# First loads in the order of use, two more banks for the third tile, the norm's steps at set places, and tables moved later, in a decoder trunk on one core

## The chip, the cores and the metric

The kernel runs on one core of one Trainium2 chip. The core has five engines with a queue each: TensorE (PE, with its weight loads PEld), VectorE (DVE), ScalarE (ACT), GpSimd (POOL) and SyncE (SP), which here only issues DMAs. Operands lie in SBUF, matmuls write to PSUM, which has eight banks of 512 float32 columns. The metric is the device time of one launch in microseconds (us); lower is better.

## The reference, cut to what matters

A trunk of two layers over 256 tokens of width 1024, in float32. Each layer has a SwiGLU feed-forward block, a mixer, and a second such block; the change touches what stands around the first block.

```python
def rms_norm(x, g):
    y = xf * lax.rsqrt(jnp.mean(xf * xf, axis=-1, keepdims=True) + EPS)
    return y * g

def swiglu(x, w_gate, w_up, w_down):
    return (jax.nn.silu(x @ w_gate) * (x @ w_up)) @ w_down      # 1024 -> 2816 -> 1024

for layer in range(2):
    if layer == 1:
        shared_kv = shared_moba_kv(h, positions, kv_norm_g, w_kv, k_norm_g)
    h = h + 0.5 * swiglu(rms_norm(h, ffn1_norm_g[layer]), ...)
    hn = rms_norm(h, mix_norm_g[layer])
    # layer 0: convolution module and attention to a memory of 256 rows
    # layer 1: attention over shared_kv (rotary, causal) and attention to the memory
    h = h + concatenate([primary, mem_out]) @ w_o[layer]
    h = h + 0.5 * swiglu(rms_norm(h, ffn2_norm_g[layer]), ...)
```

## The kernel before, in words

Everything is held transposed: channels on the partitions, the 256 tokens on the free axis. All weights come in one stream of chunks of 128 x 2048 float32 (1 MB) that SP loads in the order of use into three buffers (`raw`). Each chunk has two halves of 1024 columns, and each half is split in two: ACT rounds it (`wh`, L186), DVE takes the rest (`wl`, L190). A product with a tile of 128 x 128 weights is then three products in two matmuls (`mm2`, the "triple" of the title): `wh` on both parts of y side by side (512 columns), and `wl` on y's high part (256 columns). Four buffers hold `wh` halves and four `wl` halves.

The four feed-forward blocks are called a, b, c, d (`ffn`). Such a block has 22 tiles j of 128 hidden channels; a tile is a gate pass and an up pass of eight triples each (one for each k, the tile of input channels), into one PSUM bank each (`ag`, `au`, or `bg`, `bu` and so on). Four banks of the tag "mm" turn in rotation; two more have the tag "sc" and two the tag "aux". A bank comes free when ACT has copied its one half (`ags0c`, L237) and DVE has added the halves (`ags`, `ah`, L239). Then DVE scales the gate with the norm (L331), ACT applies Silu (L333), and the product with the up half is split again into `hs` (L336 to L338), the input of the down pass (`ao`).

The RMS norm of a block is applied after its gate product. The squares are summed over the channels (`aacc`), two small matmuls give means as columns (`mean_cols`, `anrp`), DVE and GpSimd make the reciprocal roots (`anr`), and `bcast_rows` spreads them over the partitions with two transposes (`anbp`) and a copy (`anb`). Before, the mean is taken after tile 0 of the block and the rows are made inside tile 2 (`TURN_J`), after the first matmul of triple 4 (`TURN_K`); where a turn is put inside a triple, its transposes stand between the triple's two matmuls.

The beginning is special. Warm-up matmuls (`WARM`) run on constants. x and the first chunk are loaded in pieces, two of x's from ACT's queue, and y is x times the gain, made tile by tile by ACT and DVE by turns (`scaled_split`). Tiles 0 and 1 of block a run together: the first two chunks hold, for each k, the four weight tiles of `ag0, au0, ag1, au1`. The squares of x stand on ACT beside it.

`prepare` is called before each tile of block a from tile 2 on. At tile 5 it loads the vectors, the positions, the gains and the memory, makes tables (masks in bf16, cosine and sine), squares the memory and sums it on GpSimd (`macc`); at tile 9 it makes the memory's keys and values (`mkv`). In the down passes of a, b and c a few transposes are placed that nobody reads (`unread`, at `pauses`).

A tile scheduler sets the order of the instructions of each engine from the program's order and its own costs; DMAs of SP run in the order of its queue. Everything after tile 15 of block a keeps its order on all engines apart from the places that the diff names.

Of the kernel before, what the change touches and what calls it, by code (L numbers as in the profile page):

```python
# [40 lines left out]
WARM = 12  # L41
# [12 lines left out]
TURN_J = 2  # L54
TURN_K = 4
# [30 lines left out]
def tile_kernel(ctx: ExitStack, tc: tile.TileContext, w, xT, memT, pos, vec, hg, const, out):  # L86
# [27 lines left out]
    nc.sync.dma_start(x[:, :2], xT[:, :2])  # L114
    nc.sync.dma_start(raw0[:, :HC // 2], w[0][:, :HC // 2])
    nc.scalar.dma_start(x[:, 4:6], xT[:, 4:6])
    nc.sync.dma_start(x[:, 2:4], xT[:, 2:4])
    nc.sync.dma_start(raw0[:, HC // 2:HC], w[0][:, HC // 2:HC])
    nc.scalar.dma_start(x[:, 6:], xT[:, 6:])
    nc.sync.dma_start(raw0[:, HC:], w[0][:, HC:])  # L120
# [109 lines left out]
    def mm_group2(o, y, turn=None):  # L230
        for k, wt in enumerate(tiles_of(1)):
            mm2(o, wt, y, k, k == 0, k == KD - 1, turn if k == TURN_K else None)

# [87 lines left out]
    def ffn(name, y, acc, nexts, store=False, both=False, hook=None, after=None, hook_down=None, r=None, turns=(),  # L321
            pauses=(), n_pause=2):
# [4 lines left out]
        turns = list(turns)  # L327
        halves = {}

# [10 lines left out]
        for j in range(KF):  # L340
# [4 lines left out]
            if first and j == 0:  # L345
# [7 lines left out]
                nc.scalar.dma_start(cst, const)  # L353
# [14 lines left out]
            else:  # L368
                pg, pu = psum(f"{name}g{j}"), psum(f"{name}u{j}")
                if j == 0:  # L370

                    wts = [list(tiles_of(1)) for _ in range(2)]
                    for ks in (range(KD - 1), (KD - 1,)):
                        for o, wt in zip((pg, pu), wts):
                            for k in ks:
                                mm2(o, wt[k], y, k, k == 0, k == KD - 1)
                else:
                    turn = None
                    if j == TURN_J and rb is None:
                        def turn():  # L380
                            state["rb"] = bcast_rows(name + "nb", r)
                    elif j >= TURN_J and turns:
                        turn = turns.pop(0)
                    mm_group2(pg, y, turn)
                    mm_group2(pu, y)
            if j == 0 and r is None:
                r = rstd_cols(name + "nr", acc)
            if rb is None and j < TURN_J:
                halves[j] = both_halves(f"{name}gs{j}", pg, "g"), both_halves(f"{name}h{j}", pu, "h")
                continue  # L390
            if rb is None:
                rb = state["rb"]
            for i in sorted(halves):
                gated(i, *halves.pop(i), rb)
            gated(j, both_halves(f"{name}gs{j}", pg, "g"), lambda: both_halves(f"{name}h{j}", pu, "h"), rb)
        if after:
            tables(after)
        def unread():

            pk = psum(f"{name}pk", "aux", 2)  # L400
            for i in range(n_pause):
                transp(pk[:, i * P:(i + 1) * P], ident, ident)

# [3 lines left out]
        for m in range(KD):  # L407
# [294 lines left out]
    for k in range(KD):  # L702
        scaled_split(y, x[:, k], k, V_FFN1, k % 2 == 1)
    kv0 = []

    def prepare(j):
# [3 lines left out]
        if j != 5:  # L710
            return
        nc.sync.dma_start(vt[:, V_TAP:], vec[:, V_TAP:])
        nc.sync.dma_start(pt, pos)
        nc.sync.dma_start(gt, hg)
        nc.sync.dma_start(mT, memT)
        nc.vector.tensor_copy(identb, ident)
        nc.vector.tensor_tensor(ident2, ident[:, :HALF_CH], ident[:, HALF_CH:], op=ALU.add)
        nc.vector.tensor_copy(maskb, cst[:, C_MASK:C_MASK + P])

        for g, n in ((G_MQ, 2), (G_Q, 1)):  # L720
            gn = gt[:, g * HD:(g + n) * HD]
            nc.vector.tensor_scalar(gn, gn, -1.0, None, op0=ALU.mult)

        posf = cp.tile([P, NT], F32, name="posf")
        nc.vector.tensor_copy(posf, pt)
        ang = cp.tile([P, NT, HALF], F32, name="ang")
        for i in range(NT):
            nc.vector.tensor_scalar(ang[:, i], cst[:, C_FREQ:C_FREQ + HALF], posf[:, i:i + 1], None, op0=ALU.mult)
        for shift, dst in ((0.25, cosT), (0.0, sinT)):
            kk = tp.tile([P, NT, HALF], F32, name="kk", tag="kk")  # L730
            nc.vector.tensor_scalar(kk, ang, 1.0 / TWO_PI, shift, op0=ALU.mult, op1=ALU.add)
            nc.vector.tensor_scalar(kk, kk, ROUND, ROUND, op0=ALU.add, op1=ALU.subtract)
            rr = tp.tile([P, NT, HALF], F32, name="rr", tag="rr")
            nc.vector.scalar_tensor_tensor(rr, kk, -PI_1, ang, op0=ALU.mult, op1=ALU.add)
            nc.vector.scalar_tensor_tensor(rr, kk, -PI_2, rr, op0=ALU.mult, op1=ALU.add)
            nc.vector.scalar_tensor_tensor(rr, kk, -PI_3, rr, op0=ALU.mult, op1=ALU.add)
            if shift:
                nc.vector.tensor_scalar(rr, rr, TWO_PI / 4, None, op0=ALU.add)
            nc.vector.tensor_scalar(rr, rr, 3.1415925, -3.1415925, op0=ALU.min, op1=ALU.max)
            nc.scalar.activation(dst[:, :, HALF:], rr, AF.Sin)  # L740
            if shift:
                nc.vector.tensor_copy(dst[:, :, :HALF], dst[:, :, HALF:])
            else:
                nc.vector.tensor_scalar(dst[:, :, :HALF], dst[:, :, HALF:], -1.0, None, op0=ALU.mult)

# [14 lines left out]
    def diagonals(m):  # L760
        for i in range(m * 4 * SHIFTS // KD, (m + 1) * 4 * SHIFTS // KD):
# [5 lines left out]
                    pauses=((1, 12),))  # L767
# [243 lines left out]
    (ykv, y), acc = ffn("b", y, acc, (V_KV, V_FFN1 + KD), pauses=((1, 12),), n_pause=1)  # L1011
# [9 lines left out]
    (y,), acc = ffn("c", y, acc, (V_MIX + KD,), after=AF.Exp, r=rkv, turns=turns, pauses=((1, 12), (4, 4)))  # L1021
# [40 lines left out]
    ffn("d", y, acc, (), store=True)  # L1062
# [126 lines left out]
```

## Time and profile before

| what | value |
|---|---|
| runs | 993.52, 994.16, 994.66 us (median 994.16) |
| profiled execution | 996.29 us, of which the span 994.2 |
| PE busy | 979.8 us (99%) |
| DVE, ACT, POOL busy | 734.3, 593.1, 128.4 us |
| HBM read, written | 171.43 MB, 1.05 MB |
| mean granted clock of TensorE | 0.993 |

Times in the trace are counted from the start of the span. The granted clock is 1 at 2.4 GHz and 0.5 at 1.2 GHz. A timeline row gives start, length, engine, line, operation, what it writes and reads, how many were merged, and in brackets the idle time of its engine before it with what ended it; matmuls are pipelined, so that starts and not lengths give their pace.

### The profile page before, as it was taken

How to read it: one execution, taken by the hardware profiler on the slowest of the kernel's cores; microseconds unless marked ns; L12 is line 12 of the kernel's file. 1: busy time of each engine (PE TensorE's matmuls, PEld its weight loads, DVE VectorE, ACT ScalarE, POOL GpSimd, SP SyncE). 2: the span in 40 equal slices, each digit the busy share in tenths (PEclk: the TensorE clock that was granted, in tenths of full speed). 3: DMA queues.
4: the chain of work that ended last, by engine and by line, in shares of the span. 5: the costliest groups of instructions: out<-in, count | busy, mean ns of one | idle time of the engine just before them, and what ended most of it. 6: DMA issues, size and time to landing. Idle time of an engine off the chain costs nothing.

```text
span 994.2 us, 15549 instructions
## 1 busy us (share of the span) xinstructions
PE 979.8 (99%) x5791; PEld 851.8 (86%) x5791; DVE 734.3 (74%) x1322; ACT 593.1 (60%) x1151; POOL 128.4 (13%) x150
## 2 busy tenths in 40 slices
PE   8999999999999999999999999999998999999998
PEld 6888888898779888888888888888995798888887
DVE  7887776679967877777776877767787588777663
ACT  6676578757666655555556655555555656555542
POOL 0202000128813000000122000000152030000000
PEclk9999999999999999999999999999997999999999
DMA  9555554533324555554554555555541055555560
GB/s 328 196 189 197 176 205 170 206 134 128 104 108 175 206 192 190 175 205 171 194 188 173 199 179 199 183 194 187 174 174 78 3 189 212 191 186 196 177 225 22
DMA packets 26427, 173.47 MB, mean 174 GB/s; under 512 B 3184, under 2 KB 4592, under 8 KB 6000
## 3 DMA queue, kind: packets, MB, share of 16 engines
q1 hardware_dynamic: 25776, 171.79, 49.1%
q8 instruction: 45, 0.74, 0.3%
q10 hardware_dynamic: 576, 0.70, 0.2%
q14 instruction: 30, 0.25, 0.1%
HBM read 171.43 MB, written 1.05 MB: 173 GB/s over the span
## 4 chain that ended last, share of the span: by engine, by line
PE 90%; ACT 3%; DVE 3%; POOL 2%; DMA 1%; issue 1%; SPq 0%; ACTq 0%; POOLq 0%; DVEq 0%
PE cg L150 7%; PE bg L150 6%; PE bu L150 6%; PE do L150 6%; PE ao L150 6%; PE bo L150 6%; PE co L150 6%; PE dg L150 6%; PE cu L150 6%; PE du L150 6%; PE au L150 5%; PE ag L150 5%; PE kv L150 3%; PE oao L150 2%; PE obo L150 2%; PE mkv L150 2%
## 5 line engine op out<-in xcount | busy, mean ns | idle before, releaser
L186 ACT ACTIVATE wh<-raw 128x1024 fp32r<-128x1024 f32 (+1 forms) x307 | 324.1, 1057 | 309.2 <-PE dg L150 27.7
L190 DVE TENSOR_TENSOR wl<-raw,wh 128x1024 fp32r<-128x1024 f32 (+1 forms) x307 | 377.5, 1231 | 174.9 <-ACT wh L186 173.7
L150 PE MATMUL ag<-y,wh 128*128 128x512 f32 x176 | 64.0, 399 | 3.1 <-ACT wh L186 2.9
L150 PE MATMUL au<-y,wh 128*128 128x512 f32 x176 | 63.6, 397 | 1.3 <-DVE ags L239 1.3
L150 PE MATMUL bg<-oay,wh 128*128 128x512 f32 x176 | 63.5, 399 | 0.0
L150 PE MATMUL bu<-oay,wh 128*128 128x512 f32 x176 | 63.4, 398 | 0.0
L150 PE MATMUL dg<-oby,wh 128*128 128x512 f32 x176 | 62.5, 393 | 0.0
L150 PE MATMUL cg<-by,wh 128*128 128x512 f32 x176 | 62.3, 393 | 0.0
L150 PE MATMUL du<-oby,wh 128*128 128x512 f32 x176 | 62.3, 392 | 0.0
L150 PE MATMUL cu<-by,wh 128*128 128x512 f32 x176 | 62.2, 392 | 0.0
L150 PE MATMUL ao<-ahs,wh 128*128 128x512 f32 (+1 forms) x198 | 62.0, 369 | 0.0
L150 PE MATMUL do<-dhs,wh 128*128 128x512 f32 (+1 forms) x198 | 61.9, 369 | 0.0
L150 PE MATMUL co<-chs,wh 128*128 128x512 f32 (+1 forms) x198 | 61.9, 369 | 0.0
L150 PE MATMUL bo<-bhs,wh 128*128 128x512 f32 (+1 forms) x198 | 61.9, 369 | 0.0
L150 PE MATMUL ao<-ahs,wl 128*128 128x256 f32 x176 | 49.7, 283 | 0.0
L150 PE MATMUL co<-chs,wl 128*128 128x256 f32 x176 | 49.7, 283 | 0.0
L150 PE MATMUL do<-dhs,wl 128*128 128x256 f32 x176 | 49.7, 283 | 0.0
L150 PE MATMUL bo<-bhs,wl 128*128 128x256 f32 x176 | 49.6, 283 | 0.0
L150 PE MATMUL ag<-y,wl 128*128 128x256 f32 x176 | 49.6, 283 | 0.0
L150 PE MATMUL au<-y,wl 128*128 128x256 f32 x176 | 49.5, 282 | 0.0
L150 PE MATMUL bg<-oay,wl 128*128 128x256 f32 x176 | 49.5, 281 | 0.0
L150 PE MATMUL cg<-by,wl 128*128 128x256 f32 x176 | 49.5, 281 | 0.0
(1001 smaller groups left out, 2441.2 us busy)
## 6 DMA issues: line engine op xcount, KB each, us to landing
raw<-in_w SPq DMA_DIRECT2D x158, 1024.0 KB, 4.8
raw<-in_w SPq DMA_DIRECT2D x5, 512.0 KB, 7.4
mT<-in_memT SPq DMA_DIRECT2D x1, 1024.0 KB, 8.3
out<-x SPq DMA_DIRECT2D x8, 128.0 KB, 1.7
x<-in_xT SPq DMA_DIRECT2D x2, 256.0 KB, 4.5
x<-in_xT ACTq DMA_DIRECT2D x2, 256.0 KB, 5.3
raw<-in_w SPq DMA_DIRECT2D x2, 256.0 KB, 5.1
gt<-in_hg SPq DMA_DIRECT2D x1, 192.0 KB, 6.3
```

Source lines behind the costliest of these rows:

```text
L150: return in_order("P", nc.tensor.matmul(*a, **k))
L186: state["act"] = nc.scalar.activation(wh[:, s], raw[:, s], AF.Copy)
L190: state["dve"] = nc.vector.tensor_tensor(wl[:, s], raw[:, s], wh[:, s].bitcast(F32), op=ALU.subtract)
```

## The change

The loads of x and of the first chunk are issued by SP alone, in the order in which they are used: one tile of x, the 512 columns for it, the next of both, then larger pieces. The first two chunks are split in halves of 512 columns throughout. DVE instead of ACT makes y for even tiles. The sums of tile 2 of block a go to the two "sc" banks, and their halves are added after the norm's rows are there. A plan says for each block in which tile, pass and triple the mean, the rows and other turns stand: block a has the mean in tile 2 and the rows in tile 3, block b's rows come one triple later. The memory's squares move from tile 5 to tile 8, the masks to tile 12, the cosine and sine tables to tile 14; their loads stay at tile 5. The unread transposes go, and two of the twelve warm-up matmuls. The load of the constants is put behind the last split of the first two chunks.

```diff
-WARM = 12
+WARM = 10
...
-    nc.sync.dma_start(x[:, :2], xT[:, :2])
-    nc.sync.dma_start(raw0[:, :HC // 2], w[0][:, :HC // 2])
-    nc.scalar.dma_start(x[:, 4:6], xT[:, 4:6])
-    nc.sync.dma_start(x[:, 2:4], xT[:, 2:4])
-    nc.sync.dma_start(raw0[:, HC // 2:HC], w[0][:, HC // 2:HC])
-    nc.scalar.dma_start(x[:, 6:], xT[:, 6:])
-    nc.sync.dma_start(raw0[:, HC:], w[0][:, HC:])
+    q = HC // 2
+    for tiles, cols in ((slice(0, 1), slice(0, q)), (slice(1, 2), slice(q, HC)), (slice(2, 4), slice(HC, CH)),
+                        (slice(4, KD), None)):
+        nc.sync.dma_start(x[:, tiles], xT[:, tiles])
+        if cols is not None:
+            nc.sync.dma_start(raw0[:, cols], w[0][:, cols])
...
-        q = HC // 2 if n == 0 and h == 0 else HC
+        q = HC // 2 if n < 2 else HC
...
-                nc.scalar.dma_start(cst, const)
+                behind(nc.scalar.dma_start(cst, const), state["act"])
...
-                pg, pu = psum(f"{name}g{j}"), psum(f"{name}u{j}")
+                at = ("sc", 2) if first and j == 2 else ()
+                pg, pu = psum(f"{name}g{j}", *at), psum(f"{name}u{j}", *at)
...
-                    mm_group2(pg, y, turn)
-                    mm_group2(pu, y)
+                    mm_group2(pg, y, planned(j, "g"))
+                    mm_group2(pu, y, planned(j, "u"))
...
-                    mm2(po, next(it), hs, k, k == 0, k == KF - 1, unread if (m, k) in pauses else None)
+                    mm2(po, next(it), hs, k, k == 0, k == KF - 1)
...
-        scaled_split(y, x[:, k], k, V_FFN1, k % 2 == 1)
+        scaled_split(y, x[:, k], k, V_FFN1, k % 2 == 0)
...
-        if j != 5:
-            return
+        if j == 12:
+            nc.vector.tensor_copy(identb, ident)
...
+        if j == 14:
+            posf = cp.tile([P, NT], F32, name="posf")
...
+        if j == 5:
+            nc.sync.dma_start(vt[:, V_TAP:], vec[:, V_TAP:])
+            nc.sync.dma_start(pt, pos)
+            nc.sync.dma_start(gt, hg)
+            nc.sync.dma_start(mT, memT)
+        if j != 8:
+            return
         macc = tp.tile([P, SEQ], F32, name="macc", tag="macc", bufs=1)
...
-                    pauses=((1, 12),))
+                    plan={(2, "u", 1): "mean", (3, "g", 3): "rows"})
...
-    (ykv, y), acc = ffn("b", y, acc, (V_KV, V_FFN1 + KD), pauses=((1, 12),), n_pause=1)
+    (ykv, y), acc = ffn("b", y, acc, (V_KV, V_FFN1 + KD), plan={(2, "g", 5): "rows"})
...
-    (y,), acc = ffn("c", y, acc, (V_MIX + KD,), after=AF.Exp, r=rkv, turns=turns, pauses=((1, 12), (4, 4)))
+    (y,), acc = ffn("c", y, acc, (V_MIX + KD,), after=AF.Exp, r=rkv,
+                    plan={(2 + i, "g", 4): turn for i, turn in enumerate(turns)})
...
-    ffn("d", y, acc, (), store=True)
+    ffn("d", y, acc, (), store=True, plan={(2, "g", 4): "rows"})
```

The first place is ACT's queue at the beginning, from the first y on. `wh0_0` is the first half of the first chunk, `sq0` the squares of x. Before:

```order
L275 ACTIVATE y0_110<-x_74,vt_71 128x256
L186 ACTIVATE wh0_0_139<-raw0_95 128x512
L353 DMA cst_70<-in_const 128x264
L275 ACTIVATE y0_110<-x_74,vt_71 128x256
L357 ACTIVATE sq0_226<-x_74 128x256 x4
L275 ACTIVATE y0_110<-x_74,vt_71 128x256
L357 ACTIVATE sq0_226<-x_74 128x256 x2
L275 ACTIVATE y0_110<-x_74,vt_71 128x256
L357 ACTIVATE sq0_226<-x_74 128x256 x2
L186 ACTIVATE wh0_0_139<-raw0_95 128x512
L186 ACTIVATE wh0_1_161<-raw0_95 128x1024
```

And now:

```order
L366 ACTIVATE sq0_230<-x_74 128x256
L183 ACTIVATE wh0_0_137<-raw0_93 128x512
L272 ACTIVATE y0_108<-x_74,vt_71 128x256
L366 ACTIVATE sq0_230<-x_74 128x256
L183 ACTIVATE wh0_0_137<-raw0_93 128x512
L272 ACTIVATE y0_108<-x_74,vt_71 128x256
L366 ACTIVATE sq0_230<-x_74 128x256 x2
L183 ACTIVATE wh0_1_159<-raw0_93 128x512 x2
L272 ACTIVATE y0_108<-x_74,vt_71 128x256 x2
L366 ACTIVATE sq0_230<-x_74 128x256 x4
L183 ACTIVATE wh1_0_184<-raw1_181 128x512 x2
```

Between the splits of the first two pieces stood three y and eight squares; now it is one of each, and the rest is spread over the following pieces.

The second place is DVE's queue where tiles 2 and 3 of block a are brought out of PSUM. `ags` and `ah` are the added halves of gate and up, `anb` the norm's rows, `wl5_0` the first half of the sixth chunk. Before:

```order
L190 TENSOR_TENSOR wl4_1_420<-raw4_397,wh4_1_419 128x1024
L716 CAST identb_127<-cst_70 128x128
L717 TENSOR_TENSOR ident2_133<-cst_70 128x64
L718 CAST maskb_128<-cst_70 128x128
L722 TENSOR_SCALAR gt_72<-gt_72 128x128
L336 TENSOR_TENSOR ah1_259<-ah1_259,as1_318 128x256
L722 TENSOR_SCALAR gt_72<-gt_72 128x64
L331 TENSOR_TENSOR ags2_325<-ags2_325,anb_282 128x256
L725 CAST posf_462<-pt_73 128x2
L338 TENSOR_TENSOR ahs_134<-ah0_251,ahs_134 128x256
L190 TENSOR_TENSOR wl5_0_524<-raw5_521,wh5_0_523 128x1024
L728 TENSOR_SCALAR ang_464<-cst_70,posf_462 128x8
```

And now:

```order
L187 TENSOR_TENSOR wl4_1_424<-raw4_401,wh4_1_423 128x1024
L312 COPY anb_328<-anbp_325 128x256
L340 TENSOR_TENSOR ags0_244<-ags0_244,anb_328 128x256
L340 TENSOR_TENSOR ags1_252<-ags1_252,anb_328 128x256
L345 TENSOR_TENSOR ah0_248<-ah0_248,as0_360 128x256
L236 TENSOR_TENSOR ags2_373<-ag2_258,ags2c_371 128x256
L345 TENSOR_TENSOR ah1_256<-ah1_256,as1_366 128x256
L340 TENSOR_TENSOR ags2_373<-ags2_373,anb_328 128x256
L187 TENSOR_TENSOR wl5_0_466<-raw5_463,wh5_0_465 128x1024
L187 TENSOR_TENSOR wl5_1_486<-raw5_463,wh5_1_485 128x1024
L347 TENSOR_TENSOR ahs_132<-ah0_248,ahs_132 128x256
L236 TENSOR_TENSOR ags3_387<-ag3_310,ags3c_385 128x256
```

The tables are gone from here, the copy of the rows now stands behind the fifth chunk's splits instead of the fourth's, and tile 2 is brought out only after it.

The third place is SP's queue at the beginning. Before:

```order
L114 DMA x_74<-in_xT 128x512
L115 DMA raw0_95<-in_w 128x512
L117 DMA x_74<-in_xT 128x512
L118 DMA raw0_95<-in_w 128x512
L120 DMA raw0_95<-in_w 128x1024
L163 DMA raw1_181<-in_w 128x1024
```

And now:

```order
L115 DMA x_74<-in_xT 128x256
L117 DMA raw0_93<-in_w 128x512
L115 DMA x_74<-in_xT 128x256
L117 DMA raw0_93<-in_w 128x512
L115 DMA x_74<-in_xT 128x512
L117 DMA raw0_93<-in_w 128x1024
L115 DMA x_74<-in_xT 128x1024
L160 DMA raw1_181<-in_w 128x1024
```

The first piece of x is half as large, and the second half of x, which ACT's queue loaded, stands behind the whole first chunk.

## Rows read from the trace of the kernel before

**Rows 1.** The page: busy time by engine, and the chain's shares.
```profile
PE 979.8 (99%) x5791; PEld 851.8 (86%) x5791; DVE 734.3 (74%) x1322; ACT 593.1 (60%) x1151; POOL 128.4 (13%) x150
...
PE 90%; ACT 3%; DVE 3%; POOL 2%; DMA 1%; issue 1%; SPq 0%; ACTq 0%; POOLq 0%; DVEq 0%
```

**Rows 2.** Waits of PE: for whom, us in total, times, longest.
```profile
PE ag L150 <- ACT wh L186: 2.9, 2, 2.5
PE ab2s L150 <- ACT q1T L466: 1.8, 1, 1.8
...
PE am10pp L153 <- ACT am11p L577: 1.3, 1, 1.3
```

**Rows 3.** Windows: length, busy us by engine, granted clock, DMA share, GB/s.
```profile
0.00:6.41 6.41, 4.54 (x13) 1.54 (x13) 2.19 (x10) 2.68 (x5) 0.20 (x4) 1.00 0.69 214
6.41:10.58 4.17, 1.66 (x9) 1.28 (x9) 3.59 (x10) 4.17 (x13) 0.00 (x0) 1.00 1.01 351
10.58:15.20 4.62, 4.62 (x18) 3.96 (x18) 4.04 (x4) 3.43 (x4) 0.00 (x0) 0.64 1.02 352
15.20:25.00 9.80, 9.67 (x57) 8.44 (x56) 8.37 (x13) 5.10 (x8) 0.70 (x1) 0.99 0.96 380
```

**Rows 4.** Timeline of PE, and a pass of sixteen in the chain.
```profile
6.41 0.50 PE L150 MATMUL ag<-y,wh 128*128 128x512 f32 x1 [0.42 <-ACT wh L186]
...
10.58 0.50 PE L150 MATMUL ag<-y,wh 128*128 128x512 f32 x1 [2.51 <-ACT wh L186]
...
38.50 0.50 PE L150 MATMUL au<-y,wh 128*128 128x512 f32 x1 [1.25 <-DVE ags L239]
...
41.38 0.39 PE L150 MATMUL ag<-y,wh 128*128 128x512 f32 x1
...
330.81 2.83 PE bu L150 x16
```

**Rows 5.** Timeline of ACT and DVE in the opening.
```profile
4.74 0.51 ACT L275 ACTIVATE y<-x,vt 128x256 fp32r<-128x256 f32 x1 [1.11 <-DMA vt<-in_vec]
...
5.13 0.88 DVE L276 SCALAR_TENSOR_TENSOR y<-x,vt,y 128x256 fp32r<-128x256 f32 x2
...
5.72 0.63 ACT L186 ACTIVATE wh<-raw 128x512 fp32r<-128x512 f32 x1 [0.47 <-DMA raw<-in_w]
...
9.91 2.66 ACT L186 ACTIVATE wh<-raw 128x512 fp32r<-128x512 f32 x3
...
13.11 1.06 ACT L186 ACTIVATE wh<-raw 128x1024 fp32r<-128x1024 f32 x1 [0.54 <-DMA raw<-in_w]
```

**Rows 6.** The issue of the second piece; DMA issues of 0 to 30 us.
```profile
2.12 0.43 SPq L118 DMA_DIRECT2D raw<-in_w  x1
...
raw<-in_w SPq DMA_DIRECT2D x2, 256.0 KB, 5.1
```

**Rows 7.** The costliest split group of DVE; timeline before and in the stall.
```profile
L190 DVE TENSOR_TENSOR wl<-raw,wh 128x1024 fp32r<-128x1024 f32 (+1 forms) x307 | 377.5, 1231 | 174.9 <-ACT wh L186 173.7
...
34.45 0.96 DVE L331 TENSOR_TENSOR ags<-ags,anb 128x256 f32<-128x256 f32 x1
...
36.89 2.01 POOL L285 TENSOR_TENSOR macc<-macc,mq 128x256 f32<-128x256 f32 x2 [0.80 <-ACT mq L284]
...
37.44 0.69 DVE L728 TENSOR_SCALAR ang<-cst,posf 128x8 f32<-128x8 f32 x1
...
38.03 0.41 DVE L239 TENSOR_TENSOR ags<-ag,ags3c 128x256 f32<-128x256 f32 x1
```

**Rows 8.** Timeline of PE at the unread transposes of block a.
```profile
159.54 0.39 PE L150 MATMUL ao<-ahs,wh 128*128 128x512 f32 x1
...
160.10 0.39 PE L150 MATMUL ao<-ahs,wh 128*128 128x512 f32 x1
```

**Rows 9.** Windows in the attention of layer 1.
```profile
752.59:759.42 6.83, 6.52 (x28) 3.65 (x29) 6.27 (x27) 2.64 (x11) 1.22 (x2) 0.50 0.33 140
...
762.83:766.25 3.42, 3.42 (x18) 1.70 (x16) 1.15 (x4) 0.00 (x0) 0.00 (x0) 0.50 0.00 0
```

More of the change, by code (lines that the diff above doesn't have):

```diff
@@ L53 @@
 TURN_AT = 2
-TURN_J = 2
-TURN_K = 4
 Q_AT = 6
@@ L228, in mm_group, with mm_group2 @@
             mm3(o[:, :SEQ], wt, y, k, k == 0, k == KD - 1)
-    def mm_group2(o, y, turn=None):
+    def mm_group2(o, y, turns):
         for k, wt in enumerate(tiles_of(1)):
-            mm2(o, wt, y, k, k == 0, k == KD - 1, turn if k == TURN_K else None)
+            mm2(o, wt, y, k, k == 0, k == KD - 1, turns.get(k))
     def both_halves(name, o, tag):
@@ L319, in new_acc, with ffn @@
         return tp.tile([P, SEQ], F32, name=name, tag="acc")
-    def ffn(name, y, acc, nexts, store=False, both=False, hook=None, after=None, hook_down=None, r=None, turns=(),
-            pauses=(), n_pause=2):
+    def ffn(name, y, acc, nexts, store=False, both=False, hook=None, after=None, hook_down=None, r=None, plan=None):
+        plan = plan or {}
+        rows_at = [j for (j, _, _), what in plan.items() if what == "rows"]
         hs = cp.tile([P, KF, 2, SEQ], F32R, name=name + "hs", tag="hs")
@@ L326, in ffn, with mean, rows, planned @@
         rb = None if r is None else bcast_rows(name + "nb", r)
-        turns = list(turns)
         halves = {}
+        norm = {"r": r}
+        def mean():
+            norm["r"] = rstd_cols(name + "nr", acc)
+        def rows():
+            norm["rb"] = bcast_rows(name + "nb", norm["r"])
+        def planned(j, which):
+            return {k: {"mean": mean, "rows": rows}.get(what, what) for (jj, w_, k), what in plan.items()
+                    if (jj, w_) == (j, which)}
         def gated(j, g, h, rb):
@@ L377, in ffn @@
                 else:
[L378 to L383, printed above, removed]
-                    mm_group2(pg, y, turn)
-                    mm_group2(pu, y)
[L386 to L389, printed above, removed]
+                    mm_group2(pg, y, planned(j, "g"))
+                    mm_group2(pu, y, planned(j, "u"))
+            if j == 0 and "mean" not in plan.values() and r is None:
+                mean()
+            if rb is None and j < rows_at[0]:
+                halves[j] = pg, pu
+                if j < 2:
+                    halves[j] = both_halves(f"{name}gs{j}", pg, "g"), both_halves(f"{name}h{j}", pu, "h")
                 continue
             if rb is None:
-                rb = state["rb"]
+                rb = norm["rb"]
+            halves[j] = pg, pu
             for i in sorted(halves):
-                gated(i, *halves.pop(i), rb)
-            gated(j, both_halves(f"{name}gs{j}", pg, "g"), lambda: both_halves(f"{name}h{j}", pu, "h"), rb)
+                g, h = halves.pop(i)
+                if i > 1 or not rows_at:
+                    g, h = both_halves(f"{name}gs{i}", g, "g"), (lambda i=i, h=h: both_halves(f"{name}h{i}", h, "h"))
+                gated(i, g, h, rb)
         if after:
             tables(after)
[L398 to L402, printed above, removed]
         ys = [(y_both if both else y_tiles)(f"{name}y{i}") for i in range(len(nexts))]
@@ L709, in prepare @@
             kv0.extend(mem_kv(0, my, rm))
-        if j != 5:
-            return
[L712 to L744, printed above, removed]
```

25 lines of the change are left out of this document (added).

## The prediction

> **What bounds the kernel now.** I read the page first: TensorE is busy for 99% of the span, and the chain that ended last is 90% PE [rows 1]. The reader is to see that no other engine sets the pace as a whole, so a change pays only where TensorE stands still or runs at its low clock. The waits of PE come next: 2.9 us on ScalarE's weight split (ACT wh), 1.8 and 1.3 in the attention [rows 2]. The windows then show where the first loss lies: from 10.58 to 15.20 the granted clock is 0.64 [rows 3]; as it is 0.5 or 1, about 3.3 of these 4.6 us ran at 1.2 GHz and the rest at 2.4, so some 1.7 us were lost there. Before it PE had stood still. PE's timeline has the idle times: first real matmul at 6.41, 2.51 us idle before 10.58 (until ACT had split the next piece of weights) and 1.25 us before 38.50 [rows 4]. From 6.41 to the sixth tile's first matmul at 41.38 are 34.97 us, of which 2.51 + 1.25 + 1.7 = 5.5 are lost. A gate or up pass of 16 matmuls takes 2.83 us [rows 4], a tile of two passes 5.65, five tiles 28.25; the sums and rows of the norm make up the remaining 1.2.
>
> The 2.51 us are a matter of order. ACT splits the first 512 columns at 5.72, then has eleven short instructions of y and squares in its queue, six of which need the second half of x, and comes to the next 512 columns only at 9.91 [rows 5]. These had been issued at 2.12, and such a piece takes 5.1 us to land [rows 6].
>
> **The change part by part.** The sum is made on the profiled execution (996.29 us, span 994.2; 2.1 us lie around it) and taken off the median of the runs, 994.16: the 2.1 us between the two are in both kernels.
>
> *Start.* The first matmul needs the first y and the first split. y waited for vt (ACT starts at 4.74, released by vt), and its low part was ready at 5.13 + 0.44 = 5.57; the split was ready at 5.72 + 0.63 = 6.35 [rows 5]. vt stays first on its queue. Ahead of the first weights on SP there is now one tile of x (128 KB) instead of two, and the two loads of x on ACT's queue no longer run beside them. If that does not help at all, the split stays at 6.35 (gain 0); if it helps fully, y sets the start, at 5.55. I take 5.7, nearer to y's end, since of the bytes that shared this time most now come later: **0.7 us gained** (0 to 0.9). The page "DMA: Bandwidth & Descriptors" of the Trainium skill (Anatomy of one DMA) speaks against small loads: about 2 us of each are fixed, so that by its fit, an estimate for a path other than this one, halving 256 KB takes off only 0.3 us. By that the start would gain 0.3 and the sum be 0.4 less; the rows have 5.1 us for 256 KB under load and no load of 128 KB, so they don't decide it.
>
> *Idle in the opening.* In the new ACT order each piece's split stands behind the y that goes with it. One k of the opening (four pairs of matmuls) is 4 x 0.353 = 1.41 us of PE, so from 5.7 on k = 1 is due at 7.1, k = 2 at 8.5, k = 4 at 11.4. The bytes up to the piece for k = 4 are 36 KB of vt, 1 MB of x, 1 MB and 512 KB of weights, 2.6 MB. Before, 1.37 MB moved up to 6.41 and 1.46 MB from there to 10.58 [rows 3], so 2.6 MB are read at about 10 and landed 1 us later. ACT needs 0.63 for a half split [rows 5] and has four squares ahead of it, to 11.4: PE gets k = 4 at 12.0 and waits 0.6. The last piece (k = 6, due at 15) landed before 13.11 [rows 5]. So 0.6 us instead of 2.51: **1.9 gained** (0.5 if each of four pieces is 0.35 later than this; 2.5 if none waits).
>
> *Clock.* With waits of 0.6 instead of 2.51 I expect 2.4 GHz from the first real matmul on: **1.7 gained** (0 to 1.7). Two of twelve warm-up matmuls go; ten still end near 5.4, 0.3 us before the work. The Trainium skill's "TensorE: Matmul & The Clock Gate" (Part 1) says that the activity check runs free and isn't reset when a kernel starts, so that one kernel has more or fewer slow matmuls from run to run; by it not every run of before pays the 1.7 us, and with half of that term the sum would be 5.5. The three runs lie within 1.14 us, which neither shows nor excludes it.
>
> *The stall before 38.50.* It ended with VectorE, which there had table instructions (0.69 for eight numbers a partition) and gate products stretched from about 0.4 to 0.96, while GpSimd added the memory's squares [rows 7]. Both leave this place, and the third tile's sums go to two other banks, so that the sixth tile (g5, u5) waits for the fourth's release and none for the third's. TensorE is there 5.5 us sooner, though. Along VectorE's new queue: the opening's last split ends near 14.9 (13.1, two half splits on ACT, one on DVE); then 2.2 us of square sums (1792 columns at a split's 1.23 per 1024), six splits and four short instructions of 0.41 [rows 7], to 26.1. The copy of the norm's rows waits for their transposes after 20 of the fourth tile's 32 matmuls: 5.7 + 0.6 + 11.3 + 5.65 + 0.8 + 3.5 + 0.4 = 28.0, done at 28.4. Then eight short ones and two splits to the release of g3 at 34.1, and four short ones and a split to u3 at 37.0. PE wants them at 5.7 + 0.6 + 28.25 + 1.2 = 35.8 and 38.6. With a slack of 1.6: **1.25 gained** (a loss of 1.0 if VectorE is 2.6 later than that).
>
> *Pauses.* Seven transposes that nobody reads go. Where two of them stood, the next pair of matmuls began 0.56 us after the one before, not 0.35 [rows 8], so 0.105 each: **0.75 gained** (0 if PE then waits for a split instead).
>
> *At nothing:* the memory's squares on ACT and their seven sums on GpSimd (up to 1.0 each [rows 7]) end near 55 by their queues, and the matmul that reads them stands in the second half of the ninth tile, near 57. The tables' 23 instructions go to tiles 12 and 14, where VectorE needs about 4.9 of a tile's 5.65 us (two splits, six short ones) and two tiles' banks lie between. b's rows one pair later: PE waits for nothing there. If this cover is gone, up to 1.5 lost.
>
> Sum 0.7 + 1.9 + 1.7 + 1.25 + 0.75 = 6.3, from 994.16: **987.8 us**.
>
> **Rivals.**
> *VectorE or a landing is late again.* For it: a slack of 1.6 us behind a sum of thirty instructions. Against: the tables and GpSimd's sums leave. Then the stall comes back, with up to 2.2, and part of the idle stays: 989.5 to 992.
> *The clock's gain goes elsewhere.* In the attention 6.83 and 3.42 us ran at 0.5 [rows 9], around idle times of 1.3 and 1.8 us [rows 2]. The work gets there 6 us sooner; if the check then falls otherwise on these idle times, 3.4 us more at 1.2 GHz cost 1.7 (989.5), as much less gives 986.1.
> *One queue doesn't carry it (slower).* All x and weights stand on SP now, and the sixth tile's weights are 8.7 MB down its queue with the tables and the memory. If SP's queue alone moved 190 GB/s they would be there at 2 + 45.7 = 47.7, 6.3 behind the 41.38 of now: less 0.75 of pauses, 999.7. It decides from about 220 GB/s down. Against: 380 GB/s from 15.20 to 25.00, nearly all on SP's queue [rows 3].
> *The order isn't the cause.* If the landing and not ACT's order held the second piece until 9.9, only the pauses and the stall go: 992.2. Against: 2.12 + 5.1 is 7.2.
>
> **How the numbers follow.** The forecast has 0.60, with 986.3 to 989.4 by its own bounds; the late VectorE 0.14, the clock worse 0.09 or better 0.08, the order not the cause 0.05, the one queue 0.04. A range that leaves 2 in 10 out runs from 985.8 to 990.8. A measurement of this kernel can tell about 0.2% (2 us) from no change, so faster is below 992.2: the forecast, both clock cases and nearly all of the late VectorE, 0.91; the order not the cause lies at the edge, 0.05 within; slower 0.04.
>
> **What would show it.** Right: first matmul before 6.0, no idle of PE over 1 us before 40, clock 1.00 from 6 to 25, the sixth tile's first matmul near 35.8, and the rest of the trace as before, some 6 us earlier. Wrong: an idle of PE at the fifth or sixth tile that ends with DVE, a stretch at 1.2 GHz in the opening, more of it in the attention, or splits of the second chunk that wait for their load beyond 14.

## The result, and the profile after

The kernel after took 988.05 us (median of four runs, 987.62 to 988.82) against 993.84 for the kernel before in the same series: a ratio of 0.9942 [0.9925, 0.9959] (the bracket is a 95% interval). That is 5.8 us, where 6.3 were forecast. It was timed twice more, on other chips or at other times: 990.85 (988.78 to 993.03), ratio 0.9958 [0.9942, 0.9974], and 988.68 (987.52 to 990.2), ratio 0.9941 [0.9927, 0.9955]. The first of these two lies 2 to 3 us above the others and spreads over 4 us, though its interval overlaps theirs; what makes the kernel's time move like this is the main thing the experiments explain.

The profiled execution of after took 988.82 us, with a span of 987.0 against 994.2. Its page answers [rows 1]: PE is busy for 4.0 us less, and has a larger share of the chain.

```profile
PE 975.8 (99%) x5782; PEld 849.8 (86%) x5782; DVE 733.3 (74%) x1325; ACT 593.5 (60%) x1154; POOL 129.7 (13%) x150
...
PE 92%; ACT 2%; DVE 2%; POOL 2%; DMA 1%; issue 1%; SPq 0%; POOLq 0%; ACTq 0%; DVEq 0%
```

The waits of PE in after (for whom, us in total, times, longest), beside [rows 2]: the two waits in the attention are the same, that of the opening fell from 2.9 to 1.2.

```profile
PE ab2s L147 <- ACT q1T L470: 1.8, 1, 1.8
...
PE am10pp L150 <- ACT am11p L581: 1.3, 1, 1.3
PE ag L147 <- ACT wh L183: 1.2, 2, 0.9
```

PE's timeline in after, beside [rows 4]: first real matmul at 5.50 (before 6.41), two short idle times, and none ahead of the fifth tile's up pass, where before had the 1.25 us (now 33.65, was 38.50). The sixth tile's first matmul is at 36.42 (before 41.38). Of the tables and GpSimd's sums in [rows 7] nothing is left there: GpSimd adds the memory's squares from 43.80 on.

```profile
5.50 0.83 PE L147 MATMUL ag<-y,wh 128*128 128x512 f32 x1
...
9.97 0.50 PE L147 MATMUL ag<-y,wh 128*128 128x512 f32 x1 [0.88 <-ACT wh L183]
...
13.32 0.50 PE L147 MATMUL ag<-y,wh 128*128 128x512 f32 x1 [0.29 <-ACT wh L183]
...
33.65 0.39 PE L147 MATMUL au<-y,wh 128*128 128x512 f32 x1
...
36.42 0.39 PE L147 MATMUL ag<-y,wh 128*128 128x512 f32 x1
...
39.20 0.39 PE L147 MATMUL au<-y,wh 128*128 128x512 f32 x1
```

The fourth tile's two sums (gate and up) left their PSUM banks when these two additions ended, at 34.83 and 37.30 (DVE):

```profile
34.41 0.42 DVE L236 TENSOR_TENSOR ags<-ag,ags3c 128x256 f32<-128x256 f32 x1
...
36.88 0.42 DVE L236 TENSOR_TENSOR ah<-au,ah3c 128x256 f32<-128x256 f32 x1
```

The windows of after, beside [rows 3] and [rows 9] (length, busy us and instructions by engine, granted clock, DMA share, GB/s): no stretch at 1.2 GHz is left in the opening, and two of 3.42 us are in the attention, where before had 6.83 and 3.42.

```profile
5.50:9.97 4.47, 3.60 (x17) 2.77 (x16) 2.82 (x7) 3.08 (x8) 0.00 (x0) 1.00 0.97 343
9.97:13.32 3.35, 3.05 (x17) 2.52 (x17) 3.35 (x9) 3.19 (x9) 0.00 (x0) 1.00 1.03 419
13.32:19.02 5.70, 5.70 (x32) 5.00 (x33) 5.70 (x9) 3.67 (x6) 0.00 (x0) 1.00 0.98 377
747.01:750.43 3.42, 3.23 (x16) 2.33 (x16) 3.42 (x17) 2.00 (x8) 0.75 (x2) 0.50 0.65 271
757.25:760.67 3.42, 3.42 (x18) 2.29 (x16) 2.33 (x10) 1.56 (x6) 0.00 (x0) 0.50 0.01 2
```

ACT and DVE in the opening of after, beside [rows 5]: y starts at 3.54 (was 4.74), the first split at 4.81 (was 5.72). The split at 9.29 is that of k = 2 (the third of the eight tiles of input channels) and waited for its load. Below it, from the DMA issues of 0 to 30 us, the row that answers [rows 6]: 4.0 us to landing, not 5.1.

```profile
3.54 0.35 DVE L270 TENSOR_SCALAR y<-x,vt 128x256 fp32r<-128x256 f32 x1 [1.96 <-DMA vt<-in_vec]
...
4.81 0.63 ACT L183 ACTIVATE wh<-raw 128x512 fp32r<-128x512 f32 x1 [1.02 <-DMA raw<-in_w]
...
9.29 1.15 ACT L183 ACTIVATE wh<-raw 128x512 fp32r<-128x512 f32 x2 [0.82 <-DMA raw<-in_w]
```

```profile
raw<-in_w SPq DMA_DIRECT2D x2, 256.0 KB, 4.0
```

The pairs of matmuls where the unread transposes stood [rows 8] now follow each other at 0.34 us (it was 0.56):

```profile
154.59 0.39 PE L147 MATMUL ao<-ahs,wh 128*128 128x512 f32 x1
...
154.93 0.40 PE L147 MATMUL ao<-ahs,wh 128*128 128x512 f32 x1
```

All profiles of this study can be taken apart in the same three pieces, read from the timelines: the start up to the memory's first sums (mkv), the attention from am10's transposes to the first sum of ob, and the rest of the span. "Low" is time at 1.2 GHz (start, attention); x[2:4] is when the load of x's third and fourth tiles (256 KB) landed; times in us, of the profiled execution, and the median of all runs at the end.

```
kernel              x[2:4]  third tile  sixth   mkv    attention  low        rest    span   median
before               6.89    22.67      41.38  64.02    25.15   3.4, 10.2   905.03   994.2
after                7.33    19.02      36.42  59.06    23.69   0,    6.8   904.25   987.0  988.05
e1 start alone       8.24    21.44      39.59  62.30    22.64   0,    3.4   905.06   990.0  992.39
e2 old start         7.61    22.45      39.81  62.45    21.85   3.4,  3.4   904.30   988.6  990.11
e3 mm banks          9.59    22.44      39.52  62.16    23.07   0,    6.8   904.27   989.5  989.23
e5 tables back       9.93    22.13      42.11  66.75    22.64   6.8,  3.4   904.21   993.6  992.82
e6 after again       9.60    21.78      39.20  61.84    25.12   3.4, 10.2   904.24   991.2  990.85
e7 two queues        5.09    18.71      36.14  58.78    23.44   0,    3.4   904.28   986.5  988.42
e8 swap              8.09    19.85      37.28  59.92    20.81   0,    3.4   904.27   985.0  986.10
e9 order only        7.62    19.38      38.49  61.60    22.76   0,    3.4   904.24   988.6  989.77
e10 combo            5.23    19.26      36.71  59.35    20.59   0,    0     904.26   984.2  985.81
e11 combo, fill      5.19    18.80      36.20  58.84    20.60   0,    0     904.26   983.7  985.41
e12 after, 3rd time  7.57    19.33      36.75  59.39    22.64   0,    3.4   904.27   986.3  988.68
e13 fill, 2nd time   5.25    18.93      36.33  58.96    20.58   0,    0     904.23   983.8  985.45
```

The rest is 905.0 to 905.1 where the seven unread transposes are left in and 904.2 to 904.3 where they are gone. So everything that differs lies in the start, in the attention, and in 0.78 us of transposes. From before to after that is 4.96 + 1.46 + 0.78 = 7.2, the difference of the spans. The 1.46 are not the change's: after had 23.69 us of attention in one profile and 25.12 and 22.64 in two others (e6, e12).

One thing differs that no edit asked for: in e2 and e3 the scheduler put ScalarE's q1T ahead of two of the four instructions of ab1p that stand before it in after, so that TensorE waits 0.95 and 0.84 us ahead of ab2's scores and not 1.76. With as much time at 1.2 GHz, e2 has 21.85 us of attention against e12's 22.64, e3 23.07 against after's 23.69: some 0.6 to 0.8 us that aren't their edits'.

### The profile page after: what moved, and what is told of

Its sections match the earlier page's. It is cut to its first block, busy times and chain, and to the rows that moved or that the text cites. A ratio compares the mean times of both kernels' runs of the same rounds, so it can differ in the third digit from the quotient of the medians.

```text
span 987.0 us, 15539 instructions
## 1 busy us (share of the span) xinstructions
PE 975.8 (99%) x5782; PEld 849.8 (86%) x5782; DVE 733.3 (74%) x1325; ACT 593.5 (60%) x1154; POOL 129.7 (13%) x150
## 3 DMA queue, kind: packets, MB, share of 16 engines
HBM read 171.43 MB, written 1.05 MB: 175 GB/s over the span
## 4 chain that ended last, share of the span: by engine, by line
PE 92%; ACT 2%; DVE 2%; POOL 2%; DMA 1%; issue 1%; SPq 0%; POOLq 0%; ACTq 0%; DVEq 0%
PE cg L147 7%; PE bg L147 6%; PE bu L147 6%; PE do L147 6%; PE co L147 6%; PE bo L147 6%; PE ao L147 6%; PE dg L147 6%; PE cu L147 6%; PE du L147 6%; PE ag L147 6%; PE au L147 6%; PE kv L147 3%; PE oao L147 2%; PE obo L147 2%; PE mkv L147 2%
## 5 line engine op out<-in xcount | busy, mean ns | idle before, releaser
L187 DVE TENSOR_TENSOR wl<-raw,wh 128x1024 fp32r<-128x1024 f32 (+1 forms) x310 | 377.9, 1222 | 171.0 <-ACT wh L183 170.2
L147 PE MATMUL bu<-oay,wl 128*128 128x256 f32 x176 | 49.4, 281 | 0.0
L147 PE MATMUL dg<-oby,wl 128*128 128x256 f32 x176 | 49.4, 281 | 0.0
```

The source lines that it names most:

```text
L147: return in_order("P", nc.tensor.matmul(*a, **k))
```

## The experiments

**The start alone (e1) and everything but the start (e2).** e1 is the kernel before with the new loads, warm-ups, y, splits and the later constants; e2 is after with those of before.

```
e1, on before (e2, on after, is the same lines the other way round; cuts are marked ...):
-WARM = 12
+WARM = 10
-nc.sync.dma_start(x[:, :2], xT[:, :2])
-...
+for tiles, cols in ((slice(0, 1), slice(0, q)), ...): nc.sync.dma_start(...)
-scaled_split(..., k % 2 == 1)
+scaled_split(..., k % 2 == 0)
-q = HC // 2 if n == 0 and h == 0 else HC
+q = HC // 2 if n < 2 else HC
-nc.scalar.dma_start(cst, const)
+behind(nc.scalar.dma_start(cst, const), state["act"])
```

> The kernel before with only the new opening: ordered first loads on one queue, the y of even pieces on VectorE, half splits in the first two chunks, ten warm-ups, the constants behind the splits. Tables, memory squares, banks, the norm's mean and rows and the seven pauses stay as before. My theory (the opening and VectorE's later queue are separate terms): TensorE reaches the third tile about 3.6 us sooner, as in the kernel after (19.02 against 22.67), but VectorE still has the tables in its queue, so the stall ahead of the sixth tile comes out longer than 1.25 us, by 0.5 to 3; sum 990.5 to 993, I take 991.5. Rival (the opening is all of it, VectorE's relief was not needed): 988 to 989.5, with no idle over 1.3 us ahead of the sixth tile. Rival (one queue and the order bring nothing by themselves): 993 to 994.

> The kernel after with the opening of before: loads on two queues in the old order, old parity of y, half splits only in the first piece, twelve warm-ups. Theory: idle of about 2.5 us near 8 to 10.5, a stretch at the low clock behind it, third tile near 22.7, the stall ahead of the sixth tile stays gone, no unread transposes: 988.05 + 3.65 = 991.7 (991 to 992.5). Rival (the stall and the pauses were worth nothing by themselves, all came from the opening): 993 to 994. Rival (the relief of VectorE does most): 989 to 990.

e1: ratio 0.9974 [0.9964, 0.9984]; e2: 990.11, ratio 0.9947 [0.9932, 0.9961]. In e1 TensorE's first matmul came 1.16 us earlier and no stretch at 1.2 GHz followed, but it waited 1.01 us for the sum of squares ahead of the third tile, and the idle time that VectorE ends stayed ahead of the fifth tile's up pass (PE's timeline of e1, below): together 1.85 us of waiting for VectorE, against 1.25 before. The third tile came 1.23 us earlier and mkv 1.72. I had expected the growth in the stall itself, which is 0.84; part of the new waiting stands earlier, at the norm's mean. The median is 992.39, near what I took (991.5). e2 has the old idle time (2.59) and the stretch at 1.2 GHz back, no stall at the sixth tile, and mkv at 62.45, 3.39 behind after; its median is only 1.4 to 2.1 us behind that of two of after's series and 0.7 ahead of e6's, and its interval overlaps all three. I had expected 991 to 992.5. Some 0.8 us of that miss are ScalarE's order in the attention (21.85), said above. So what the new opening adds to the rest shows in the traces, but not clearly in the medians.

```profile
20.97 0.61 PE L149 MATMUL anrp<-onec,aacc 128*128 128x1 f32 x4 [1.01 <-DVE aacc L360]
...
36.67 0.50 PE L149 MATMUL au<-y,wh 128*128 128x512 f32 x1 [0.84 <-DVE ags L238]
```

**The banks (e3) and the tables (e5).**

```
e3:
-at = ("sc", 2) if first and j == 2 else ()
+at = ()
e5, three conditions in prepare (the masks, the tables, the memory's squares):
-if j == 12:
+if j == 5:
-if j == 14:
+if j == 5:
-if j != 8:
+if j != 5:
```

> The kernel after, but the third tile's two sums in the ring of four banks again, not in two banks of their own. My theory in the prediction had a slack of 1.6 us with the two banks; without them the fourth, fifth and sixth tile each want a bank one tile sooner, and the first tiles' banks come free only when VectorE has the norm's rows (28.7 us): an idle of 0.5 to 2 us ahead of the fifth or sixth tile, 988.6 to 990. Rival (moving the tables away is enough, the banks add nothing): 987.8 to 988.3 and no idle of TensorE there.

> The kernel after, but the tables' instructions, the copies of constants and the memory's squares stand at the sixth tile's place in the program again (two banks kept). Theory: VectorE has about twenty short instructions ahead of the sixth tile's weight splits, GpSimd adds the memory's squares beside them, and TensorE waits 1 to 3 us ahead of the sixth tile: 989 to 991. Rival (the two banks give enough cover): within 0.3 of 988.05.

e3: 989.23, ratio 0.9944 [0.9929, 0.9959], the same as after within the intervals. That lies in the range I gave, but not for my reason: it has no idle time at the fifth or sixth tile; its later start comes from x[2:4] at 9.59 and from the norm's mean, which the scheduler puts ahead of the third tile without the banks (1.05 us of waiting for the sum of squares). But with that its third tile starts at 22.44, 3.4 us after that of after, so VectorE had that much more time: e3 shows that the stall can stay away without the two banks when TensorE comes late, not that they are worth nothing when it comes early. e5: 992.82 (990.4 to 996.15), ratio 0.9976 [0.9962, 0.999], 3.6 us behind e3 in the same series, of which some 0.6 are that order in e3's attention. What moved back does it: TensorE waits 2.37 us for VectorE at the sixth tile, and 3.4 us at 1.2 GHz follow. The masks, the tables and the memory's squares moved together; no run parts them. PE's timeline of e5:

```profile
42.11 0.47 PE L147 MATMUL ag<-y,wh 128*128 128x512 f32 x1 [2.37 <-DVE ags L236]
```

e3 and e5 have the loads and ACT order of after, and yet idle times of 1.66 and 2.46 us at k = 1, which after doesn't have. That asked for after itself once more.

**After again (e6), and x[2:4] on the other queue (e7).**

```
e6: after, unchanged
e7, in effect (in the kernel this line is one turn of a loop):
-nc.sync.dma_start(x[:, 2:4], xT[:, 2:4])
+nc.scalar.dma_start(x[:, 2:4], xT[:, 2:4])
```

> The kernel after, unchanged, beside the next two on one chip. In the four kernels measured so far the same first loads gave different landings: x[2:4] landed at 7.33 in the profile of after, at 8.24, 9.59 and 9.93 in the others, and TensorE stood still for 1.2 us in all in the first and for 2.1 to 2.9 in the others. Theory A (the landing of the new first loads varies from execution to execution): the median is 988 to 990 and the profile shows x[2:4] anywhere from 7 to 10. Theory B (it was the other edits or that chip): 988.05 within 0.5 and x[2:4] near 7.3.

> The kernel after, but x[2:4] is loaded by ScalarE's queue behind vt, all else in the same order on SP's. With one queue the first 8 us moved 220 to 310 GB/s between 4 and 8 us, with the old two queues 360 to 417. Theory (the one queue with small loads is the slower start): over 330 GB/s between 4 and 8 us, x[2:4] lands before 6.6 and the second half of the first chunk before 9, TensorE's idle times before 15 us add up to less than 1.2 us, and the median is 0.5 to 1.5 below the kernel after beside it. Rival (the landing is set by the bytes ahead of it, not by the queue): landings within 0.5 us of the kernel after and the same median.

e6: 990.85, ratio 0.9958 [0.9942, 0.9974], above the 988 to 990 of theory A, which it otherwise bears out. In its profile x[2:4] landed at 9.60; VectorE has the y of that piece in its queue ahead of the second low split (L187), which it had all data for, and TensorE stood still for 1.89 us until that split was done. A stretch at 1.2 GHz followed, so that the start was 2.8 us longer than in the first profile of after. Timeline of DVE and PE in e6, and the window from there on:

```profile
9.63 0.36 DVE L270 TENSOR_SCALAR y<-x,vt 128x256 fp32r<-128x256 f32 x1 [3.35 <-DMA x<-in_xT]
9.90 0.69 DVE L187 TENSOR_TENSOR wl<-raw,wh 128x512 fp32r<-128x512 f32 x1
...
10.64 0.39 PE L147 MATMUL ag<-y,wl 128*128 128x256 f32 x1 [1.89 <-DVE wl L187]
```

```profile
10.64:15.72 5.08, 4.76 (x17) 3.88 (x18) 4.78 (x12) 4.67 (x12) 0.00 (x0) 0.66 1.02 401
```

A load of this kernel counts as landed when sixteen parts of it have, and the trace has the time of each. Of x[2:4] in e6 the first landed at 5.67, the eighth at 6.58, the fifteenth at 8.17, the last at 9.60; in the first profile of after 5.59, 6.32, 7.16 and 7.33. The middle ones hardly differ from one execution to the next; one or two parts fall behind, and the loads behind them in the queue carry the delay on (second half of the first chunk: eighth at 8.22, last at 10.99). In e7 the sixteen parts of x[2:4] lie between 4.35 and 5.09: it was issued at 1.18 (2.58 in e6), and its load takes 3.9 us instead of 7.0. The issue rows of e6 and of e7 (KB each, us to landing):

```profile
x<-in_xT SPq DMA_DIRECT2D x1, 256.0 KB, 7.0
```

```profile
x<-in_xT ACTq DMA_DIRECT2D x1, 256.0 KB, 3.9
```

e7: 988.42, ratio 0.9939 [0.9922, 0.9955], 2.4 below e6 where I expected 0.5 to 1.5; idle times of 0.61, 0.16 and 0.28, and no stretch at 1.2 GHz in the start. By the medians alone it isn't told from e6 (the intervals overlap), nor from the other two series of after. The rate came out against my theory: from 4 to 6 and from 6 to 8 us it moved 285 and 271 GB/s, not over 330 (e6: 214 and 267). The first profile of after moved 250 and 312, the same on average, and had x[2:4] only at 7.33. So the rate doesn't explain the earlier landing; that x[2:4] doesn't stand behind 768 KB of the one queue, and is issued 1.4 us sooner, does. Of the idle time, the 0.61 us are mostly ScalarE's order again: in e7 the scheduler put y and squares of the next pieces ahead of the second split, whose piece had landed at 6.53 and was split at 7.18.

**The order without the new loads (e9).** After with the loads of before, the order on ScalarE set by hand.

```
in effect (what stands in <> is told in words):
+i = nc.scalar.activation(yh[:, k], ...)
+behind(i, <the split of piece k>)
+behind(nc.scalar.activation(sq[:, k], x[:, k], AF.Square), <the last split of the opening>)
```

> The kernel after with the loads of before (two queues, old order of the pieces), but with each y from the third on put by hand behind the split of its own piece on ScalarE and all squares behind the last split of the opening. It parts the order on the engines from the order of the loads. With the same loads and the scheduler's own order (e2) TensorE stood still for 2.59 us and then had 3.4 us at 1.2 GHz; the memory's sums began at 62.45. Theory (ScalarE's order made the idle time, the step of the prediction): the second piece lands near 7.9 to 8.6 and is split by 9.2, the idle times add up to 0.5 to 1.5 us, no stretch at 1.2 GHz before 40, the memory's sums begin at 59 to 60.5, 2 to 3.4 us before e2's. Rival (the old loads land too late whatever the order): an idle time of 2 us or more, 61.5 to 62.5.

989.77, ratio 0.9956 [0.9943, 0.9968]. The idle time is 0.88 instead of e2's 2.59, no stretch at 1.2 GHz follows, and the third tile starts 3.1 us earlier than in e2 with the same loads. The second piece landed at 8.53 in e9 and at 8.61 in e2; ScalarE split it at 8.55 in e9, where it stood waiting for it, and at 10.32 in e2, behind the y and squares (ACT's timeline of e9, then of e2):

```profile
8.55 0.63 ACT L184 ACTIVATE wh<-raw 128x512 fp32r<-128x512 f32 x1 [2.07 <-DMA raw<-in_w]
```

```profile
10.32 1.56 ACT L184 ACTIVATE wh<-raw 128x512 fp32r<-128x512 f32 x2
```

So ScalarE's order made the idle time. (e9 also keeps after's ten warm-ups, its half splits and its share of y between ScalarE and VectorE; the split of this piece is a half in both.) mkv is at 61.60, outside what I expected and at the place that the rival named, but not by the rival's idle time: the squares, all behind the splits, made VectorE's sums late, and the stall came back (PE's timeline of e9):

```profile
9.24 0.50 PE L148 MATMUL ag<-y,wh 128*128 128x512 f32 x1 [0.88 <-ACT wh L184]
...
38.49 0.48 PE L148 MATMUL ag<-y,wh 128*128 128x512 f32 x1 [1.59 <-DVE ags L237]
```

**The attention (e8), and all together (e10, e11).**

```
e8:  before go(pairs[p + 2], 2):   +if p == TURN_AT: go(pairs[p - 1], 2)
e10: the edits of e7 and e8
e11: that of e10, and behind ab0's scores  +for _ in range(6): mmul(S[0][:, 3 * P:], onem, onem, start=False, stop=True)
```

> The kernel after, but in the second attention the four matmuls of am11's output stand ahead of ab2's scores, which wait 1.76 us for ScalarE: they are ready by then (VectorE's copy ends at 754.2, the idle time runs from 753.55 to 755.31). Theory: the idle time falls to about 0.7, the matmuls' 1.1 us go: 1.1 us faster than the kernel after; and if the stretch at 1.2 GHz that began at 757.26 comes from this idle time, it goes as well, 1.7 more, so 985.5 to 987. Rival (the stretch comes from the rest of the attention, with its short matmuls and the idle time of 1.3 us): only the 1.1 us. Rival (ScalarE's and VectorE's orders, which follow, make ab2 as much later): no change.

> The kernel after with both edits that helped: x[2:4] on ScalarE's queue and am11's output ahead of ab2's scores. Theory: the gains add, 988.4 less 3.0 (what the second one took off beside the same before: 986.1 against 988.8 to 993.0 of after, of which the landing is a part): 984.5 to 986, and a spread over the runs under 1.5 us, since neither the late landing nor the idle time of 1.76 us is left. Rival (in the second one's five runs the landing was a good one, so there is nothing to add): 985.8 to 986.5.

> The one before, with six multiplications of a constant that nobody reads, into unread columns of ab0's scores, where TensorE stands still for 1.33 us ahead of am10's transposes. They take 1.3 us at the full clock and hide in that idle time. Theory (the last stretch at 1.2 GHz in the attention comes from this idle time): that stretch goes, 1.7 us gained over the one before, and the mean clock of the span is 1.00. Rival (the stretch comes from the attention's small matmuls as a whole, or from idle times elsewhere): the stretch stays, the time stays or grows by up to 0.5.

e8: 986.10 (986.06 to 986.75), ratio 0.9912 [0.9894, 0.9929], below e6's interval. The idle time of 1.76 us ahead of ab2's scores is gone (timeline of PE in e8). The attention took 20.81 us. In e12, which is after itself, it took 22.64 with the stretch at 1.2 GHz at the same place as in e8, the attention's first matmuls; in e7 23.44 with the stretch behind the idle time. So by these single profiles some 1.8 are the edit and 0.8 the place of the stretch, and e12 shows that the stretch behind the idle time can be missing without the edit. The 1.8 aren't the moved matmuls alone: in e8 the scheduler also put ScalarE's q1T ahead of all four instructions of ab1p, and e2, with two of them behind it and the matmuls where they were, had 21.85.

```profile
754.82 1.49 PE L147 MATMUL am11o<-am11t,kvs 128*64 128x256 f32 x8
756.25 0.93 PE L147 MATMUL ab2s<-kvs,q1T 64*128 64x128 f32 x8
```

e10: 985.81, ratio 0.9919 [0.9905, 0.9932]; e11: 985.41, ratio 0.9912 [0.9899, 0.9926]. They don't differ by what can be measured, from each other or from e8. 985.81 lies both in my range for e10 and in the rival's, so whether x[2:4] on the other queue adds anything to e8 stays open. e11 is to take a stretch away that e10's profile no longer had, so its question stays open; in e11's runs the mean clock was 0.999 or 1.00 each time, in e10's 0.997 to 1.00. (A stretch at the first place, behind the idle time of 1.33, costs little: e8 with it 20.81, e10 without 20.59.)

**After and e11's kernel on one chip (e12, e13).**

> The kernel after once more, beside the next on one chip. Theory (the landing of x[2:4] sets its time): if the profile has it before 8, no stretch at 1.2 GHz in the opening and the memory's sums at 59 to 60; if after 9, at 61 to 62. The median lies between 988 and 991.

> The version with x[2:4] on ScalarE's queue, am11's output ahead of ab2's scores and the six unread multiplications, beside the kernel after. Theory: 985 to 986 with all runs within 1 us, 2.5 to 5 below the kernel after; x[2:4] lands before 6. Rival (its gain over the kernel after came from the chip of the earlier series): less than 1.5 below.

After: 988.68, with x[2:4] at 7.57, no stretch at 1.2 GHz in the start and mkv at 59.39. The version of e11: 985.45 (985.1 to 985.57), ratio to before 0.9906 [0.9893, 0.9919], which lies below after's 0.9941 [0.9927, 0.9955]: 3.2 us less than after, 9.0 less than before.

## Why the prediction was right, and where it was lucky

The sum came within 0.3 us of the first median (987.8 and 988.05). That much agreement is luck: the same kernel's second series has 990.85, just outside the stated range, and the difference is a landing that the prediction took as fixed. The terms, by the profiles of before and after, add up to 0.91 + 1.34 + 1.7 + 1.25 = 5.2 for the start, of which 4.96 were seen at mkv (the first two matmuls of after lost 0.3 against those of before), where 5.55 were forecast.

- **Start, 0.7 us: right.** 0.91 in after, 0.7 to 1.2 in the other profiles with the new first loads. By the Trainium skill's "DMA: Bandwidth & Descriptors" (Anatomy of one DMA) the smaller load alone would have brought 0.3, an estimate; the first split began 0.91 earlier. The two loads of x that left ScalarE's queue are in these 0.91 as well, so no run here shows the smaller load by itself.
- **Idle in the opening, 1.9 us: too large, and at the wrong place.** 2.51 became 1.17 in after, 1.3 gained. The 0.6 that I expected at k = 4 were 0.29; the other 0.88 came at k = 2, for which I had no wait: its load landed at 9.27. The step "so 2.6 MB are read at about 10 and landed 1 us later" took a load's landing from the mean rate; it is set by the slowest of its sixteen parts. With these loads on one queue the idle times of the opening add up to 1.2 to 2.9 us in seven profiles (after, e1, e3, e5, e6, e8, e12), with x[2:4] on the other queue to 0.5 to 1.4 in four (e7, e10, e11, e13). The 5.1 us to landing was the middle of two loads; the second piece itself took 5.8 and landed at 7.88. The cause that I named, ScalarE's order, is shown by e9.
- **Clock, 1.7 us: right when the idle time is short.** The stretch at 1.2 GHz was gone in after, e7, e8 and e12, and there again in e5 and e6, behind idle times of 2.46 and 1.89; behind 1.66 (e3) there was none. By the Trainium skill's "TensorE: Matmul & The Clock Gate" (Part 1) the check runs free of the kernel. The trace agrees as far as it goes: in three profiles of after the same idle times of the attention were followed by 3.4, 6.8 and 10.2 us at 1.2 GHz.
- **Stall, 1.25 us: right, and by the slack that I gave.** The sixth tile came at 36.42, not 35.8, with the start's 0.6 of idle that I had put too low; VectorE was about as much later, so the fourth tile's banks were free 1.6 us (gate) and 1.9 us (up) before they were wanted, where I had 1.6. e5 shows that the instructions moved away were needed for it, and e9 how little more it takes: with late squares 1.59 us of stall are back. What the two banks are worth stays open. In before the fifth tile's up pass waited for the fourth tile's gate sum; in after it began at 33.65, 1.2 us before that sum left its bank, so the banks may well have mattered there, and e3's TensorE came too late to show it. The new places of the mean and the rows weren't tested by themselves.
- **Pauses, 0.75 us: right.** 0.78 by the rest of the span.
- **At nothing: right.** GpSimd's last sum of the memory ended at 53.9, and the rest of the span is the same to 0.1 us in every kernel without the transposes.
- **Rivals.** "VectorE or a landing is late again" (989.5 to 992, chance 0.14) is what e6's series showed, with a landing: 990.85. Of all 17 runs of after 7 lie there (5 of e6's, 2 of e12's), so its chance was too low. "One queue doesn't carry it" fell as priced (no wait for weights at the sixth tile), but the one queue is what made x[2:4] late (e6 against e7). "The order isn't the cause" fell with e9. "The clock's gain goes elsewhere": it did both, between 22.64 and 25.12 us of attention, by the execution and not by the change.

## What to carry to other kernels

Ask of each instruction in an in-order queue which load it waits for, and what stands behind it that has its data: after's new order put a split that was ready behind a y that wasn't, and this cost 1.9 us when a load was late. Price a landing by its slowest part and not by the mean rate, and keep a load that is needed early off the queue that carries the bulk; here it landed 2.2 to 4.5 us sooner for it, though the medians don't show what that is worth. An idle time of TensorE may cost up to 1.7 us more at the low clock behind it (3.4 us at half speed), so fill it with work that is ready (e8). When an edit leaves the order to a scheduler, compare the orders of all engines before a difference is put down to the edit (e2, e3, e8). And time a change more than once before a few tenths of a per cent are believed.

## What was not expected of the hardware

- The last of a load's sixteen parts fell 3.0 to 3.4 us behind the eighth in e3, e5 and e6 (9.60 against 6.58 in e6), on the queue that carried all first loads, and by amounts that differ from execution to execution; on x[2:4] of the other queue it was 0.4 to 0.6 (e7, e10, e11, e13), but later loads of two-queue kernels have up to 2.7 (e9). The Trainium skill's "DMA: Bandwidth & Descriptors" (Issuing engines are not separate DMA queues) says that a second queue saves only the issue time; here x[2:4] landed 4.5 us earlier from the other queue than in e6 (5.09 against 9.60) and 2.2 earlier than in the first profile of after (7.33). Its earlier issue is 1.4 us of that; the rest isn't issue time, and against after it isn't the rate from 4 to 8 us either (both some 280 GB/s). What changed is its place among the loads.
- The clock fell behind an idle time of 1.9 us in one execution (e6) and not behind 1.7 in another (e3), and in the attention it fell for 3.4, 6.8 or 10.2 us with the same instructions (e12, after, e6), and for 3.4 or 0 with those of e8 (e8, e10).
- Six multiplications of 128 x 128 in f32 fitted into an idle time of 1.33 us and left the matmul behind them where it was (am10's transposes 25.2 us behind rq's sums in e10 and e11).
